# Two trunk layers on one core: GpSimd's elementwise work moves to VectorE, attention scores are computed over 128 rows, and the modulation products are shared out anew

## The chip, the cores and the metric

One core of one Trainium2 chip runs the whole program in one launch. The metric is device time in microseconds, from start to end of an execution; lower is better. TensorE (PE) multiplies, VectorE (DVE), ScalarE (ACT) and GpSimd (POOL) work elementwise, and SyncE (SP) only issues the transfers from and to memory (DMA).

## The reference, cut to what matters

384 tokens (256 latent, 128 context) of width 1024 pass through two layers. Everything is float32.

```python
def swiglu(h, w1, w3, w2):
    return (jax.nn.silu(h @ w1) * (h @ w3)) @ w2
...
m = jax.nn.silu(cond) @ w_mod[l] + b_mod[l]          # 9 vectors of 1024 for each layer and kind of token
...
h = swiglu(mod(x, 0), ffn1_w1[l], ffn1_w3[l], ffn1_w2[l])
x = layer_norm(ALPHA * x + 0.5 * m[:, :, 2] * h, ln_g[l, 0], ln_b[l, 0])
h, aux = mixer(mod(x, 1), l)
x = layer_norm(ALPHA * x + m[:, :, 5] * h, ln_g[l, 1], ln_b[l, 1])
h = swiglu(mod(x, 2), ffn2_w1[l], ffn2_w3[l], ffn2_w2[l])
x = layer_norm(ALPHA * x + 0.5 * m[:, :, 8] * h, ln_g[l, 2], ln_b[l, 2])
```

`mod(x, i)` is x(1+scale)+shift with two of the nine vectors. The mixer projects its input to pooling, to differential attention (4 heads with two softmax maps each), to neighbourhood attention (4 heads) and to three gate vectors, projects each branch to 1024 columns, adds them up under their gates and multiplies by `w_out`. Latent queries and keys of the differential attention are rotated (rope).

## The kernel before, in words

**High and low parts.** PE multiplies a rounded format (`fp32r`). Every operand of a large product is therefore split: ACT writes the rounded high part, another engine subtracts it and writes the low part, and `mm3` makes three passes (high by high, high by low, low by high). Weights come as 384 units of 128 x 1024 in one fixed order (`PLAN`), each loaded to `raw` by SP, rounded to `whi` by ACT and subtracted to `wlo` by DVE (`split_one`, L262). Ten split units are kept ahead of PE (`RING`).

**FFNs.** There are four, called FFN(layer, 0 or 1). A round j multiplies one unit each of `w1` and `w3` by the transposed input `xT` (24 passes of 384 columns each, into two banks `f`), then `glu` makes h on ACT and DVE, its high part `hhi` on ACT and its low part `hlo` on GpSimd. Up to round 16 a round also multiplies an earlier h by a unit of `w2` (18 passes of 512 columns into `acc`); the last six units of `w2` are kept for `tail`, which finishes one block of 128 tokens after the other, so that the layer norm of a block on DVE and ACT lies beside the products of the next. The first FFN begins inside `start`, which has an order of its own and computes the first 16 modulation columns.

**Modulation.** A product of the condition with 128 columns of `w_mod` (a "unit" of modulation) is done on DVE by two passes over 128 x 1024, one for each kind of token (`gemv_acc`, L306, tiles `wm` and `junk`). There are 128 units after the start. `gemv_quota` and `gemv_tick` spread them in the FFNs over "ticks" (one after each weight unit that PE uses up): 24 in each of three FFNs and 8 in the last, and each mixer takes 24.

**Residual.** `xa` keeps the normalised x without its gain and offset. `residual` (L415, L416) multiplies by the one and adds the other on GpSimd, three blocks after each layer norm but the last: in FFNs in rounds 7 to 9, in a mixer after the v projections (`rows_pass`, tile `v`).

**Mixers.** After the v projections a planner, `Jobs.emit`, takes jobs with an engine, a duration and dependencies, and fixes the order of the instructions on every engine. Priorities are `SIDE` (attention) before `UNIT` (projections, gates, output products, in their fixed order) before `SLOW` (modulation). Attention runs in 12 items with 384 keys and 6 with 128 keys for each mixer: scores (`ss`), maximum (DVE), exponential (ACT), transposes (`pt`), values (`o`). One item's scores are four passes: for each half e of a head pair one over 128 rows (`qa` holds the high part of q twice; `ka` holds the high and the low part of k) and one over 64 rows (`ql`, the low part of q, with the high part of k). q's low part and most of the rope (`u`, `kraw`) are GpSimd's, k's low part is DVE's. The chosen order is static: each engine runs its list and waits where an input is late.

Of the kernel before, what the change touches and what calls it, by code (L numbers as in the profile page):

```python
# [18 lines left out]
P = 128  # L19
# [5 lines left out]
HD = 64  # L25
# [27 lines left out]
MIX_LATENCY = 0.1, 2.0  # L53
SPLITS = 1
# [3 lines left out]
QK_LO = "GV"  # L58
# [50 lines left out]
class Jobs:  # L109
# [9 lines left out]

    def after(self, i, d):  # L120

        self.jobs[i][2].append(d)

    def emit(self, stock=None):
        n = len(self.jobs)
        rank = [0.0] * n
        for i in reversed(range(n)):
            rank[i] += self.jobs[i][1]
            for d in self.jobs[i][2]:
                rank[d] = max(rank[d], rank[i] + self.latency)  # L130
# [6 lines left out]
        while todo:  # L137
            best = None
            for i in todo:
# [3 lines left out]
                t = max([at.get(eng, 0.0)] + [end[d] + (self.dma_latency if self.jobs[d][0] == "D" else self.latency) for d in deps])  # L143
# [31 lines left out]
def trunk_kernel(ctx: ExitStack, tc: tile.TileContext, wst, wmod, wmod0, x_lat, x_ctx, cvec, cT,  # L175
# [4 lines left out]
    N_Q, N_S = 34, 21  # L180
# [305 lines left out]
    def tail(acc, accl, hT, keys, nk, gates, l, s):  # L486
# [67 lines left out]
        to_xT_ev(1, bs1, ab)  # L554
        t[2], nm[2] = ln_sum(2, acc[2], gates[1])
# [4 lines left out]
        pump(4 if s == 0 else 2)  # L560
# [8 lines left out]
    def glu(b1, b3, n, hT_hi, hT_lo):  # L569
        s = get("S", [P, n], F32, "s")  # L570
        S.activation(s, b1, AF.Silu)  # L571
        h = get("S", [P, n], F32, "h")
        V.tensor_tensor(h, s, b3, ALU.mult)  # L573
        S.copy(hT_hi, h)  # L574
        G.tensor_tensor(hT_lo, h, hT_hi.bitcast(F32), ALU.subtract)  # L575
        rel(s, h)

    def ffn(l, f, ctx_part, gate_at):
# [7 lines left out]
        j0 = N_ST if first else 2  # L586

# [7 lines left out]
        if first:  # L595
# [3 lines left out]
            gemv_quota(24, TICKS0)  # L599
        else:  # L600
            gemv_quota(min(24, len(gq)), TICKS * min(24, len(gq)))
            pair = [[take(w, l, f, h) for h in range(2)] for w in ("w1p", "w3p")]
            for c in range(2):
# [11 lines left out]
                glu(bb[0], bb[1], 256, hT[c][0][:, 0:256], hT[c][1][:, 0:256])  # L615
# [72 lines left out]
    def mix(l, ctx_part, H):  # L688
# [32 lines left out]
        gb = ln_rows(l, 0)  # L721
# [37 lines left out]
        n_gv = min(MIX_GEMV, len(gq))  # L759
# [37 lines left out]

        misc = [lambda: load("pool", 1.9, (band, cband),
# [31 lines left out]
        for i in range(first, last_u):  # L830
# [6 lines left out]
            d = add("A", .95, [raw_ld[i], d], split_hi, W_PRIO, need="W")  # L837
            d = u_lo[i] = add("V", 1.14, [d], lo, W_PRIO, free="R")
# [10 lines left out]
        def product(i, key, deps=()):  # L849
# [12 lines left out]
            for k0 in range(0, KC, PRODUCT_CUT):  # L862
                k1 = min(KC, k0 + PRODUCT_CUT)
                chain[0] = add("P", .49 * (k1 - k0), [u_lo[i], chain[0]] + list(deps), part(k0, k1), UNIT,
# [4 lines left out]
        d = None  # L869
        for k in gv:  # L870
# [10 lines left out]
            d = add("V", 1.16, [ld["wm", k], d], f0, SLOW)  # L881
            d = add("V", 1.16, [d], f1, SLOW, free="M")
# [13 lines left out]
        jobs.after(gate_d[0], add("A", .2, [d], f, free="B"))  # L896
# [31 lines left out]
        y_done = {}  # L928
        pT = [get("S", [P, T], F32, "pT") for _ in range(2)]
# [21 lines left out]
        for fc in range(2):  # L951
# [28 lines left out]
        def k_out(src, n, dep):  # L980
# [12 lines left out]
            return add("A", .2, [d], f, free="B")  # L993

        def to_y(kind, m, deps):
# [8 lines left out]
            def f():  # L1004
                box["y", kind, m] = get("S", [P, T], F32, "y")
                V.tensor_scalar(box["y", kind, m], box["yT", kind, m], gcol if kind == "b" else 1.0, None, ALU.mult)
                rel(box["yT", kind, m], ytok.pop((kind, m)))
            d = add("V", .53, [d], f, need="S", free="B S")

            def f():  # L1010
                out[m] = get("S", [P, T], F32R, "yhi"), get("S", [P, T], F32R, "ylo")
                S.copy(out[m][0], box["y", kind, m])
            d = add("A", .43, [d], f, need="S S")

            def f():
                G.tensor_tensor(out[m][1], box["y", kind, m], out[m][0].bitcast(F32), ALU.subtract)
                rel(box["y", kind, m])
            y_done[1 if kind == "b" else 2, m] = add("G", .98, [d], f, free="S")
# [626 lines left out]
```

## Time and profile before

| | us |
|---|---|
| median of 3 runs (1794.89 to 1797.36) | 1795.97 |
| the profiled execution's own time | 1795.24 |
| its span, first to last instruction | 1793.3 |

| engine | busy us | share of the span | instructions |
|---|---|---|---|
| PE matmuls | 1743.0 | 97% | 9444 |
| PE weight loads | 1619.8 | 90% | 9444 |
| DVE | 1254.2 | 70% | 1871 |
| ACT | 718.7 | 40% | 1234 |
| POOL | 365.3 | 20% | 263 |

PE is listed as busy nearly all the time, but its instructions overlap and their ends are modelled, so this share doesn't say that PE works at its full pace; the distance from one start to the next does. The other engines' shares are means over stages of different kinds: the start takes 68 us, FFN(0,0) ends at about 315, the first mixer at 638, FFN(0,1) at 906, FFN(1,0) at 1183, the second mixer at 1508.

### The profile page before, as it was taken

To read this page: it belongs to the slowest core of one execution; us is meant where nothing else is said; L and a number is where in the kernel's file an instruction comes from. 1 tells how busy PE (TensorE), PEld (TensorE's weight loads), DVE (VectorE), ACT (ScalarE), POOL (GpSimd) and SP (SyncE) were. 2 spreads that over 40 slices of the span, in tenths; PEclk is the share of its full clock that TensorE was granted. 3 is DMA by queue.
4 is the path that set the end of the run, shared out by engine and by line. 5 is a ranking of instruction groups with operands and counts; after the bars stand their busy time and mean duration, and the time that the engine had idled before them with its cause. 6 is when DMAs were issued, how large, how long until landed. Compare 5 with 4: busy or idle time off the path is not lost.

```text
span 1793.3 us, 24509 instructions
## 1 busy us (share of the span) xinstructions
PE 1743.0 (97%) x9444; PEld 1619.8 (90%) x9444; DVE 1254.2 (70%) x1871; ACT 718.7 (40%) x1234; POOL 365.3 (20%) x263
## 2 busy tenths in 40 slices
PE   7899999999999999999999999999999999999998
PEld 6799999788899999999999999978889999999997
DVE  6775656779988886776475776565998988665234
ACT  5532333355653362323353332334465445423231
POOL 4400000347210100410100320123540110023010
PEclk8999999999999999999999999999999999999999
DMA  8465553352446355465346465425244652653420
GB/s 320 143 238 186 186 188 118 105 216 95 147 177 238 138 209 197 167 223 191 118 149 223 157 223 201 153 72 183 103 143 144 250 206 99 233 176 132 143 102 35
DMA packets 88072, 301.65 MB, mean 168 GB/s; under 512 B 11058, under 2 KB 13970, under 8 KB 87956
## 3 DMA queue, kind: packets, MB, share of 16 engines
q1 hardware_dynamic: 87956, 300.09, 47.1%
q8 instruction: 74, 1.21, 0.3%
q14 instruction: 42, 0.34, 0.1%
HBM read 296.86 MB, written 3.19 MB: 167 GB/s over the span
## 4 chain that ended last, share of the span: by engine, by line
PE 84%; DVE 10%; issue 3%; ACT 1%; POOL 1%; DMA 1%; SPq 0%; DVEq 0%; ACTq 0%; POOLq 0%
PE f L214 38%; PE acc L214 24%; PE gt L214 11%; PE pj L214 4%; DVE junk L306 3%; DVE wlo L262 2%; PE v L214 2%; PE ss L214 1%; PE st L214 1%; PE f1c L214 1%; PE xTp L424 1%; DVE ka L1165 1%; PE o L214 1%; DVE u L1208 1%; DVE mx L1053 1%
## 5 line engine op out<-in xcount | busy, mean ns | idle before, releaser
L262 DVE TENSOR_TENSOR wlo<-raw,whi 128x1024 fp32r<-128x1024 f32 x379 | 488.9, 1317 | 153.8 <-ACT whi L257 153.4
L214 PE MATMUL f<-xT_hi,whi 128*128 128x384 f32 (+1 forms) x1344 | 445.2, 331 | 0.0
L214 PE MATMUL f<-xT_hi,wlo 128*128 128x384 f32 (+1 forms) x1344 | 444.9, 331 | 0.0
L214 PE MATMUL f<-xT_lo,whi 128*128 128x384 f32 (+1 forms) x1344 | 444.5, 331 | 0.0
L257 ACT CAST whi<-raw 128x1024 fp32r<-128x1024 f32 x384 | 384.2, 1047 | 11.1 <-DVE modcol L306 7.4
L306 DVE CUSTOM_DVE_ANT_0 junk<-wm,silu_bc 128x1024 bf16<-128x1024 f32 x256 | 350.7, 1370 | 3.5
L575 POOL TENSOR_TENSOR hlo<-h,hhi 128x384 fp32r<-128x384 f32 (+1 forms) x84 | 84.0, 1000 | 901.8 <-ACT hhi L574 901.8
L214 PEld LDWEIGHTS f<-xT_hi,whi 128*128 128x128 f32 x1344 | 252.7, 188 | 2.4
L214 PEld LDWEIGHTS f<-xT_lo,whi 128*128 128x128 f32 x1344 | 252.7, 188 | 2.4
L214 PEld LDWEIGHTS f<-xT_hi,wlo 128*128 128x128 f32 x1344 | 252.6, 188 | 0.0
L214 PE MATMUL acc<-whi,hlo 128*128 128x512 f32 x624 | 244.2, 391 | 0.0
L214 PE MATMUL acc<-wlo,hhi 128*128 128x512 f32 x624 | 244.0, 391 | 0.0
L214 PE MATMUL acc<-whi,hhi 128*128 128x512 f32 x624 | 244.0, 391 | 0.0
L573 DVE TENSOR_TENSOR h<-s,f 128x384 f32<-128x384 f32 (+1 forms) x84 | 45.7, 544 | 248.3 <-PE f L214 179.6
L574 ACT CAST hhi<-h 128x384 fp32r<-128x384 f32 (+1 forms) x84 | 42.5, 505 | 346.5 <-DVE h L573 346.5
L571 ACT ACTIVATE s<-f 128x384 f32<-128x384 f32 (+1 forms) x84 | 40.7, 484 | 262.0 <-PE f L214 261.9
L214 PEld LDWEIGHTS acc<-whi,hlo 128*128 128x128 f32 x624 | 117.1, 188 | 24.6
L214 PEld LDWEIGHTS acc<-whi,hhi 128*128 128x128 f32 x624 | 117.2, 188 | 22.8
L214 PEld LDWEIGHTS acc<-wlo,hhi 128*128 128x128 f32 x624 | 117.1, 188 | 22.8
L214 PE MATMUL gt<-xT_hi,whi 128*128 128x384 f32 x384 | 129.7, 338 | 0.0
L214 PE MATMUL gt<-xT_lo,whi 128*128 128x384 f32 x384 | 128.5, 335 | 0.0
L214 PE MATMUL gt<-xT_hi,wlo 128*128 128x384 f32 x384 | 128.5, 335 | 0.0
(236 smaller groups left out, 2370.9 us busy)
## 6 DMA issues: line engine op xcount, KB each, us to landing
raw<-in_wst SPq DMA_DIRECT2D x384, 512.0 KB, 3.7
wm<-in_wmod SPq DMA_DIRECT2D x128, 512.0 KB, 4.7
ld<-in_wmod SPq DMA_DIRECT2D x16, 512.0 KB, 9.5
gate<-gd SPq DMA_DIRECT2D x12, 512.0 KB, 3.9
lng<-in_lnrow SPq DMA_DIRECT2D x6, 512.0 KB, 3.9
lnb<-in_lnrow SPq DMA_DIRECT2D x6, 512.0 KB, 4.9
nab<-in_nabias SPq DMA_DIRECT2D x4, 512.0 KB, 7.3
out<-y SPq DMA_DIRECT2D x6, 256.0 KB, 2.0
```

The lines of the kernel that those rows point to most:

```text
L214: PE.matmul(out, a, b, start=start, stop=stop)
L257: S.copy(ws[i][0], raws[i])
L262: eng.tensor_tensor(ws[i][1], raw, ws[i][0].bitcast(F32), ALU.subtract)
L306: V.tensor_tensor_reduce(out=junk, in0=t, in1=silu_bc["t"][:, cd, :], scale=1.0, scalar=0.0, op0=ALU.mult, op1=ALU.add, accum_out=modcol[l ...
L424: PE.transpose(b[:, q, :], t[:, kc * P:(kc + 1) * P], ident)
L571: S.activation(s, b1, AF.Silu)
L573: V.tensor_tensor(h, s, b3, ALU.mult)
L574: S.copy(hT_hi, h)
L575: G.tensor_tensor(hT_lo, h, hT_hi.bitcast(F32), ALU.subtract)
L1053: V.reduce_max(mx, ss[:, :, :N], axis=AX.X)
L1165: KL.tensor_tensor(box["ka", kind, m][e][rs[1 - e], :], kt[rs[e], 0:384], box["ka", kind, m][e][rs[e], :].bitcast(F32), ALU.subtract)
L1208: V.tensor_tensor(u[0][o:o + 32, :], qT["b", m][i:i + 32, 0:256], rope[i:i + 32, 1, :], ALU.mult)
```

## The change

Five things are changed together.

1. Elementwise work leaves GpSimd in the FFNs and mixers: `hlo`, the residual, q's low part, the rope and the bias of the neighbourhood attention go to DVE. In `glu` the low part becomes a function `low`, which the FFN calls after the tick. The partner rows of the rope are copied out of PSUM by ACT (`rot`, four copies of 32 rows).
2. Scores: one tile `qs` holds the high part of q and its low part, each twice, so that both passes contract over 128 rows.
3. Modulation units: 42, 36, 36 and 8 in the four FFNs, 6 in the first mixer and 0 in the second.
4. In `tail` ahead of a mixer two weight units are split before the last block's layer norm, where all four were split after it.
5. The durations of the planner's jobs are other numbers, and it counts no delay between two jobs of one engine and a longer one behind PE (`PE_LAG`). The mixers' residual becomes six jobs of the lowest priority. The start is planned by the same rule, so some rows there change places.

```diff
-TICKS0, TICKS = 52, 2.1
+GEMV_TICKS = 52
+FFN_GEMV = {(0, 0): 42, (0, 1): 36, (1, 0): 36, (1, 1): 8}
-MIX_GEMV, MIX_AHEAD = 24, 10
+MIX_GEMV, MIX_AHEAD = (6, 0), 10
...
     def residual(ti, gb):
-        G.tensor_tensor(xa[ti], xa[ti], gb[0], ALU.mult)
-        G.tensor_tensor(xa[ti], xa[ti], gb[1], ALU.add)
+        for e, op in ((0, ALU.mult), (1, ALU.add)):
+            V.tensor_tensor(xa[ti], xa[ti], gb[e], op)
...
         to_xT_ev(1, bs1, ab)
+        if s == 0:
+            pump(2)
         t[2], nm[2] = ln_sum(2, acc[2], gates[1])
...
-        pump(4 if s == 0 else 2)
+        pump(2)
...
         V.tensor_tensor(h, s, b3, ALU.mult)
         S.copy(hT_hi, h)
-        G.tensor_tensor(hT_lo, h, hT_hi.bitcast(F32), ALU.subtract)
+        def low():
+            V.tensor_tensor(hT_lo, h, hT_hi.bitcast(F32), ALU.subtract)
+        return low
...
-                    glu(bb[0], bb[1], T, *hT[j])
+                    lows.append(glu(bb[0], bb[1], T, *hT[j]))
                     rel(*bb)
                 tick()
+                while lows:
+                    lows.pop(0)()
...
-                        mm(o, qq[:, t * P:(t + 1) * P], kk, True, False)
-                        mm(o, ql[r, t * P:(t + 1) * P], kk[r, :], False, True)
+                        for h in range(2):
+                            mm(o, qq[:, h, :], kk, h == 0, h == 1)
...
-            d = add("A", .95, [raw_ld[i], d], split_hi, W_PRIO, need="W")
-            d = u_lo[i] = add("V", 1.14, [d], lo, W_PRIO, free="R")
+            d = add("A", 1.05, [raw_ld[i], d], split_hi, W_PRIO, need="W")
+            d = u_lo[i] = add("V", 1.35, [d], lo, W_PRIO, free="R")
```

On DVE at the end of FFN(0,0), the rows from the last round's h to the first row of the tail stand so before (`junk` is one modulation pass; the last round's `hlo` stands on POOL):

```order
L573 TENSOR_TENSOR h_2422<-s_2420,f_418_2393 128x384
L262 TENSOR_TENSOR wlo_2427<-raw_2356,whi_2426 128x1024
L306 ISA junk,modcol_72<-wm_2360,silu_bc 128x1024
L306 ISA modcol_72 128x1
L306 ISA junk,modcol_72<-wm_2360,silu_bc 128x1024
L306 ISA modcol_72 128x1
L314 TENSOR_TENSOR modcol_72<-modcol_72,bmod 128x16
```

and so in the changed kernel:

```order
L581 TENSOR_TENSOR h_2497<-s_2495,f_436_2468 128x384
L268 TENSOR_TENSOR wlo_2501<-raw_2425,whi_2500 128x1024
L312 ISA junk,modcol_72<-wm_2466,silu_bc 128x1024
L312 ISA modcol_72 128x1
L312 ISA junk,modcol_72<-wm_2466,silu_bc 128x1024
L312 ISA modcol_72 128x1
L586 TENSOR_TENSOR hlo_2494<-h_2497,hhi_2493 128x384
```

The last round's `hlo` now stands on DVE behind one weight split and one modulation unit. In FFN(0,1) and FFN(1,0) only the weight split stands between, and in FFN(1,1) nothing.

On DVE in the tail of FFN(0,0), just ahead of the first mixer, the last block's layer norm (from `r` to `xa`) and the four weight splits behind it stand so before:

```order
L453 TENSOR_TENSOR xT_lo<-y_2621,xT_hi 128x4x128 x2
L396 TENSOR_TENSOR r_2634<-acc_750,gate_1840 128x512
...
L558 TENSOR_SCALAR xa_94<-r_2634,nm_2640,rs_2643 128x1024
L262 TENSOR_TENSOR wlo_2655<-raw_2391,whi_2654 128x1024
L262 TENSOR_TENSOR wlo_2661<-raw_2430,whi_2660 128x1024
L262 TENSOR_TENSOR wlo_2667<-raw_2658,whi_2666 128x1024
L262 TENSOR_TENSOR wlo_2673<-raw_2664,whi_2672 128x1024
```

and so in the changed kernel:

```order
L459 TENSOR_TENSOR xT_lo<-y_2695,xT_hi 128x4x128 x2
L268 TENSOR_TENSOR wlo_2709<-raw_2462,whi_2708 128x1024
L268 TENSOR_TENSOR wlo_2715<-raw_2504,whi_2714 128x1024
L402 TENSOR_TENSOR r_2720<-acc_756,gate_1889 128x512
...
L566 TENSOR_SCALAR xa_94<-r_2720,nm_2726,rs_2729 128x1024
L268 TENSOR_TENSOR wlo_2741<-raw_2712,whi_2740 128x1024
L268 TENSOR_TENSOR wlo_2747<-raw_2718,whi_2746 128x1024
```

Two splits moved ahead of the layer norm.

On PE in the first mixer, an item's scores stand so before, with the row before and after them:

```order
L214 MATMUL o_3199<-va_2681,pT_3181 128x64
L214 MATMUL ss_3202<-ka_3061,qa_3048 128x384
L214 MATMUL ss_3202<-ka_3061,ql_3187 128x384
L214 MATMUL ss_3202<-ka_3062,qa_3049 128x384
L214 MATMUL ss_3202<-ka_3062,ql_3187 128x384
L983 MATMUL kt_3219<-ident,kc_2885 128x128
```

and so in the changed kernel:

```order
L220 MATMUL o_3439<-va_2755,pT_3390 128x64
L220 MATMUL ss_3454<-ka_3239,qs_3323 128x384 x2
L220 MATMUL ss_3454<-ka_3240,qs_3323 128x384 x2
L1098 MATMUL pt_3463<-ident,p_3393 128x128
L1098 MATMUL pt_3464<-ident,p_3394 128x128
```

The count of passes stays; the two of 64 rows are gone.

## Rows read from the trace of the kernel before

**Rows 1.** Stages: us, busy us (instructions) of PE, PEld, DVE, ACT, POOL; PEclk; DMA

```profile
364.50:503.00 138.50, 132.06 (x747) 118.14 (x745) 125.60 (x230) 79.48 (x202) 61.09 (x52) 0.99 0.42 151
638.00:906.00 268.00, 268.00 (x1481) 253.13 (x1480) 174.62 (x231) 93.43 (x130) 41.74 (x28) 1.00 0.51 178
...
1234.00:1372.00 138.00, 131.21 (x743) 117.75 (x741) 125.71 (x229) 79.13 (x202) 61.21 (x52) 0.99 0.42 150
```

**Rows 2.** Chain of waits, 378 to 455 us (shares), 453 to 457.5 us (start, us)

```profile
by line: DVE wlo L262 17.9%; DVE junk L306 15.4%; issue 12.3%; DVE ka L1165 9.2%; DVE u L1208 7.7%; DVE mx L1053 6.2%; PE kb L214 5.5%; DVE ss L1052 3.3%; DVE ytok L1112 3.2%; DVE mx L1048 2.6%; DVE p L1072 2.6%; DVE cf L1071 1.9%; DVE mx L
...
455.29 0.67 PE o L214 x6
```

**Rows 3.** Chain of waits of the whole span, in FFN(0,1): start, us, what

```profile
773.29 8.34 PE f L214 x48
781.63 4.12 PE acc L214 x18
...
848.20 41.62 PE f L214 x240
```

**Rows 4.** Lines L262 and L306: count, ns min/median/max, first and last start

```profile
L262 DVE TENSOR_TENSOR wlo<-raw,whi x379: 1207/1220/3428, 15.2 to 1745.7; 128x1024 fp32r<-128x1024 f32 x190
...
L306 DVE CUSTOM_DVE_ANT_0 junk<-wm,silu_bc x256: 1208/1222/3424, 99.9 to 1595.3; 128x1024 bf16<-128x1024 f32 x128
```

**Rows 5.** Timeline where the mixers begin: start, us, engine, line, what [idle before]

```profile
333.91 2.84 DVE L558 TENSOR_SCALAR xa<-r,nm,rs 128x1024 f32<-128x1024 f32 x1
336.67 4.49 DVE L262 TENSOR_TENSOR wlo<-raw,whi 128x1024 fp32r<-128x1024 f32 x2
...
328.98 2.40 POOL L415 TENSOR_TENSOR xa<-xa,lng 128x1024 f32<-128x1024 f32 x1 [28.18 <-DMA lng<-in_lnrow]
...
336.28 2.67 POOL L416 TENSOR_TENSOR xa<-xa,lnb 128x1024 f32<-128x1024 f32 x1
...
340.08 0.50 PE L214 MATMUL v<-wlo,xT_hi 128*128 128x512 f32 x1 [4.24 <-DVE wlo L262]
...
1209.14 0.79 PE L214 MATMUL v<-wlo,xT_hi 128*128 128x512 f32 x1 [4.40 <-DVE wlo L262]
```

**Rows 6.** Stretches behind those two waits, columns as in rows 1

```profile
340.60:344.00 3.40, 3.40 (x9) 2.64 (x9) 2.83 (x3) 0.00 (x0) 0.00 (x0) 0.50 0.44 154
...
1209.10:1214.40 5.30, 5.26 (x12) 4.13 (x13) 3.39 (x3) 0.00 (x0) 0.00 (x0) 0.50 0.42 140
```

**Rows 7.** Timeline of PE, one item's scores, up to the next instruction

```profile
478.09 0.34 PE L214 MATMUL ss<-ka,qa 128*128 128x384 f32 x1
478.36 0.44 PE L214 MATMUL ss<-ka,ql 64*128 64x384 f32 x1
...
479.46 0.55 PE L1082 MATMUL pt<-ident,p 128*128 128x128 f32 x3
```

**Rows 8.** Groups on DVE, 364.5 to 503 us: busy us, mean ns | idle before

```profile
L306 DVE CUSTOM_DVE_ANT_0 junk<-wm,silu_bc 128x1024 bf16<-128x1024 f32 x21 | 31.3, 1491 | 0.1
```

**Rows 9.** Groups on POOL, whole span, columns as in rows 8

```profile
L415 POOL TENSOR_TENSOR xa<-xa,lng 128x1024 f32<-128x1024 f32 x15 | 45.0, 3001 | 75.8 <-DMA lng<-in_lnrow 56.5 <-PE xTp L424 19.3
```

**Rows 10.** Timeline at the end of FFN(0,0), DVE, ACT, POOL and PE

```profile
298.54 0.55 DVE L573 TENSOR_TENSOR h<-s,f 128x384 f32<-128x384 f32 x1 [1.40 <-PE f L214]
300.69 1.23 DVE L262 TENSOR_TENSOR wlo<-raw,whi 128x1024 fp32r<-128x1024 f32 x1 [1.59 <-ACT whi L257]
301.83 1.22 DVE L306 CUSTOM_DVE_ANT_0 junk<-wm,silu_bc 128x1024 bf16<-128x1024 f32 x1
...
304.36 0.17 DVE L314 TENSOR_TENSOR modcol<-modcol,bmod 128x16 f32<-128x16 f32 x1
...
299.61 1.05 ACT L257 CAST whi<-raw 128x1024 fp32r<-128x1024 f32 x1
...
299.78 1.01 POOL L575 TENSOR_TENSOR hlo<-h,hhi 128x384 fp32r<-128x384 f32 x1 [7.31 <-ACT hhi L574]
...
302.14 0.39 PE L214 MATMUL acc<-whi,hlo 128*128 128x512 f32 x1
```

More of the change, by code (lines that the diff above doesn't have):

```diff
@@ L863, in product @@
                 k1 = min(KC, k0 + PRODUCT_CUT)
[L864 removed]
+                chain[0] = add("P", .52 * (k1 - k0), [u_lo[i], chain[0]] + list(deps), part(k0, k1), UNIT,
                                need="" if k0 else "B", free="W" if k1 == KC else "")
             return chain[0]
[L869 removed]
+        d = v5 = None
         for k in gv:
@@ L895, in f @@
             rel(box["gT"])
-        jobs.after(gate_d[0], add("A", .2, [d], f, free="B"))
+        jobs.after(gate_d[0], add("A", .25, [d], f, free="B"))
+        d = ld["gb"]
+        for ti in range(3):
+            for e, op in ((0, ALU.mult), (1, ALU.add)):
+                def f(ti=ti, e=e, op=op):
+                    V.tensor_tensor(xa[ti], xa[ti], box["gb"][e], op)
+                    if (ti, e) == (2, 1):
+                        rel(*box["gb"])
+                d = add("V", 1.25, [d], f, SLOW, free="W" if (ti, e) == (2, 1) else "")
         neglam = cst.tile([P, 1], F32, tag=f"neglam{l}", name=f"neglam{l}")
@@ L1002, in to_y @@
             d = add("P", .4, deps, f, need="B")
[L1004 to L1018, printed above, removed]
+            split_y((1 if kind == "b" else 2, m), out, m, lambda: box["yT", kind, m], lambda: gcol if kind == "b" else 1.0, d,
+                    lambda: rel(box["yT", kind, m], ytok.pop((kind, m))), "B S")
         def item(kind, m, t, ready):
@@ L1147, in fq @@
             def fq():
-                qa = box["qa", kind, m] = [get("S", [P, 256], F32R, "qa") for _ in range(2)]
+                qs = box["qs", kind, m] = get("Q", [P, 2, 2, 256], F32R, "qs")
                 for e in range(2):
                     for r in rs:
-                        S.copy(qa[e][r, :], qT[kind, m][rs[e], 0:256])
+                        S.copy(qs[r, e, 0, :], qT[kind, m][rs[e], 0:256])
             def fk():
@@ L1230, in mix, with rotate, f @@
-            r = add("G", 1.4, [d], f, free="S S S" + " S" * (m == 3))
+                    S.copy(p[o:o + 32, :], b[i:i + 32, 0:256])
+                rel(b)
+            return add("A", 2.1 if key == "q" else 2.4, [dep], f, need="S S", free="B")
+        for m in range(4):
+            q = evac_pair("q", m, product(unit("qb", l, m), ("qb", m)))
+            k = evac_pair("k", m, product(unit("kb", l, m), ("kb", m)))
+            ko = k_out(kb_t(m)[:, 384:512], m, k)
+            def rotate(key, m=m):
+                def f():
+                    x = qT["b", m][:, 0:256] if key == "q" else box["kraw", m]
+                    out = x if key == "q" else kb_t(m)[:, 0:256]
+                    p = box["p" + key, m]
+                    V.tensor_tensor(p, p, rope[:, 1, :], ALU.mult)
+                    V.tensor_tensor(x, x, rope[:, 0, :], ALU.mult)
+                    V.tensor_tensor(out, x, p, ALU.add)
+                    rel(p)
+                    if key == "k":
+                        rel(x)
+                        if m == 3:
+                            rel(rope)
+                return f
+            r = add("V", 1.3, [q, ld["rope"]], rotate("q"), free="S")
+            r = add("V", 1.3, [k, r], rotate("k"), free="S S" + " S" * (m == 3))
```

177 lines of the change are left out of this document (82 added, 95 removed).

## The prediction

> **What bounds the kernel now.** I read the stages first, then the chain of waits in the stage where PE falls behind, then timelines at the places that the change touches. In an FFN the chain is PE alone: 24 passes of 384 columns take 4.17 us (0.174 us each), 18 of 512 columns take 4.12 us (0.229 each), and one stretch follows the other without a gap [rows 3]. Nothing on DVE, ACT or POOL shortens that. In the attention stage of a mixer it is different. There DVE is busy for 125.6 of 138.5 us [rows 1], and the chain from 378 to 455 us runs almost wholly over DVE: weight splits 18%, modulation passes 15%, score and rope pieces behind them [rows 2]. PE is listed at 132.1 us there, but count its work at full pace: 12 projections and 7 gates of 24 passes and 6 products of 6 are 492 passes of 384 columns at 0.174, so 85.6 us; 48 score passes would be 8.4 us at that pace; the other 207 of its 747 instructions start about 0.11 us apart when nothing holds them (0.67 us for 6) [rows 2], so 23 us. That is 117 us of work in 138.5 us, and the same in the second mixer's 138.0 us [rows 1]. So DVE bounds this stage, and up to 21.5 us per mixer can be had there.
>
> DVE is slow for two reasons. It does much, and it is held up: a weight split takes 1.22 us in the median and up to 3.43, a modulation pass 1.22 and up to 3.42 [rows 4]; the long ones lie beside GpSimd instructions [rows 5].
>
> **The change, part by part.**
>
> *Start of the mixers.* PE waited 4.24 and 4.40 us for a weight split [rows 5]. The split was late because the layer norm before it was: the residual ran on GpSimd from 328.98 to 338.95 us, and beside it the normalising step took 2.84 us (two-input passes of that width take 1.22 where nothing holds them) and two splits took 4.49 instead of 2.44 [rows 4, 5]. Now GpSimd is empty and two of the four splits stand ahead of the layer norm. They delay it by 2.4 us and the missing blocks give back 1.6 in the normalising step alone; the next two splits are needed only two units later, 12 passes of 0.23 us. So both waits should go. Behind them PE's granted clock stood at 0.50, the 1.2 GHz level, for 3.4 and 5.3 us [rows 6], which costs half of that, 1.7 and 2.6 us. Gain 4.24 + 4.40 + 1.7 + 2.6 = 12.9 us; between 6 (a wait of half the length stays) and 13.
>
> *Score passes.* An item's four passes take 478.09 to 479.46, so 1.37 us, where four at 0.174 would take 0.70; a full pass before a 64-row one is held too (0.27) [rows 7]. 24 items in two mixers: 0.67 x 24 = 16 us of PE time. Between 0 and 16, and part of the room counted above, not on top of it. The Trainium skill (TensorE: Matmul & The Clock Gate, section "Why this matters for your kernels") says that a matmul over fewer contraction rows takes the same time as one over 128; by that this edit gains nothing, and the rows here, at about twice the time of a full pass, don't agree.
>
> *VectorE's load in the attention stage.* Removed: 21 modulation passes of 1.49 us and their reads, about 33 us [rows 8]; the blocks on what stays. Added, with 0.42 us for 256 columns (a straight line through 0.55 for 384 and 1.22 for 1024 [rows 4, 10]): q's low part 12 x 0.42 = 5, rope 24 pieces instead of 16, so 3.4, bias 2 x 1.22 = 2.4, together 11 us. That leaves about 104 of 138.5 us. In the first mixer 2 modulation units (5 us) and the residual (6 x 1.22 = 7.3 us, which cost GpSimd 3.0 each [rows 9]) are put in between at lowest priority. So DVE falls to some 104 to 116 us, PE's 117 us become the floor, and ACT (79.5 us [rows 1]) gains rope and score copies and stays below both. The gain lies between 5 us per mixer (score passes where PE doesn't wait today, 7 or 8 of 12 items) and 21.5 (PE never waits). Three engines at 75 to 95% under static lists won't reach the floor; I take three quarters, 16 us per mixer, 32 in all.
>
> *FFNs.* GpSimd's blocks cost nothing here today (PE didn't wait), so nothing is gained. What is added: `hlo` (0.55 us for 1.01) and more modulation. One round of FFN(0,0) on DVE: h 0.55, then a wait of 1.60 until ACT has done `hhi` and the next weight's high part, splits at 1.14, `hlo` 0.58, modulation units at 2.53 [rows 10]. With 42 units in 52 ticks: 0.55 + 1.60 + 3 x 1.14 + 0.58 + 2.42 x 2.53 = 12.3 us against PE's 8.34 + 4.12 = 12.46: just fits. In the last five rounds, without `w2`, PE takes 8.32 (41.62 / 5) [rows 3]; DVE needs 10.1 us with two units and 7.5 with one. The skipped ticks fall so that three of the last four steps have two: h comes late by 1.7, 1.0, 2.7 and at last 4.4 us. PE doesn't feel that before the tail. There it wants the last `hlo` at 302.14, and GpSimd had it at 300.79 [rows 10]. Now: h starts 298.54 + 4.4 = 302.9, then 0.55 + 1.60 + 1.14 + 2.53 + 0.55 = 6.4, so 309.3, a wait of 7.2 us, and a spell at half clock of the kind above (1.7). Without the lateness the wait would be 2.8. I take 8 us lost, between 3 and 11. In FFN(0,1) and FFN(1,0) units stop five ticks before the end, the lateness is worked off, and `hlo` stands behind one split: 298.54 + 0.55 + 1.60 + 1.14 + 0.55 = 302.4, so 0.3 us lost each. The residual's 2.4 us in rounds 7 to 9 are covered by the ten units ahead of PE; without that cover they would cost up to 7 us in each.
>
> *Start, and the units' transfers.* The start's list changes by a few rows: nothing in sum, within plus or minus 2 us (one or two passes of 1.22 [rows 4] earlier or later). The extra `wm` loads raise the traffic in the FFNs, where DMA engines were busy half of the time [rows 1]: nothing.
>
> *Sum.* 12.9 + 32 - 8 - 0.6 = 36 us. Against the profiled execution's 1795.24 (span 1793.3 and 1.9 around it, 0.7 under the median of 1795.97): 1759.
>
> **Rivals.**
>
> *The attention stage stays slow.* ACT gets four copies of 32 rows for each of q and k and a second copy of q's low part, and scores wait for that longer way; only one item's scores fit at a time. For it: in 138.5 us ACT had only 79.5 busy, but it stands in every link. Against it: the chain was DVE's. Then 5 us per mixer: 12.9 + 10 - 8.6 = 14 gained, 1781.
>
> *Modulation finds its place in FFN(0,0) after all* (the lateness doesn't build up, or the last rounds have more slack): 5 to 7 us better, 1753.
>
> *Score passes stay as slow as now*, as by the skill's rule. For it: PE's first pass of an item is long too, which 64 rows alone wouldn't explain. Against it: every 128-row pass elsewhere starts 0.174 after the last. PE's floor rises by 8 us per mixer to 125; three quarters of 13.5 are 10 each, so 1771.
>
> *Slower: VectorE becomes the bound of three FFNs.* If the long passes on DVE aren't GpSimd's doing, a modulation pass stays at its mean of today (1.37, with read 1.45) and a split at 1.32 in the FFNs. Then a round of FFN(0,0) takes 0.55 + 1.60 + 4.0 + 0.58 + 2.42 x 2.9 = 13.7, 1.3 over PE's, and its last five 10.0 against 8.32: 13 x 1.3 + 5 x 1.7 = 25 us, with some 8 at the end; FFN(0,1) and FFN(1,0) lose 5 to 8 each, and in the mixers 32 shrinks to some 16. 12.9 + 16 - 33 - 13 = 17 slower, 1812. It decides from the point where a round on DVE takes longer than PE's 12.46. Against it: the medians of 1.22 lie at the minimum [rows 4], so most instances are unhindered.
>
> **How the numbers follow.** Forecast (mixers gain most, FFN(0,0) pays) 0.55, 1748 to 1770, likeliest 1759; modulation finds its place 0.14, 1753 and down to 1743; attention stays slow 0.16, about 1781 and up to 1788; scores stay slow 0.06, 1771; slower 0.06, 1800 to 1812; no change within 0.2% 0.03. A change of 0.2% (3.6 us) is about the least that can be told here. So faster 0.91, same 0.03, slower 0.06. The range of 1742 to 1786 leaves out the slower case, the unchanged one and the ends of two others.
>
> **What would show it.** Right: no wait of PE for `wlo` at `v`; an item's score passes in about 0.7 us; weight splits and modulation passes outside the start all near 1.22 us; 364 to 503 us shrinks by 10 to 20 with DVE's share lower; a PE wait of 3 to 8 us for `hlo` at the end of FFN(0,0), with the clock at 0.5 behind it, and hardly any in the next two. Wrong: gaps between `f` and `acc` inside FFNs; PE waiting for ACT's copies in attention; score passes at 0.35 us as today.

## The result

The changed kernel takes 1766.43 us (median of 4 runs, 1763.96 to 1768.49) against 1796.01 for the kernel before (4 runs, 1794.89 to 1797.36): ratio 0.9834, 95% interval 0.9817 to 0.9851. That is 29.6 us less; 36 less, 1759, were forecast. The profiled execution, the slowest of the four, took 1768.49 us with a span of 1766.8.

To see where the time went, the trace was read through PE's starts. For two matmuls that follow each other, the distance between their starts, less the distance at full pace for that width (0.1735 us for 384 columns, 0.227 for 512, 0.120 for 256, 0.109 for 128, 0.084 for 64), is time that PE lost, be it a wait, a half clock or a slow pass. Gaps under 25 ns are left out. Added up by stage (us; attention is the 138 us from the first `qc` on):

| kernel | start | end of FFN(0,0) | mixers begin | attention 1 | attention 2 | mixers end | FFN(0,1), FFN(1,0) begin | rest | lost | span |
|---|---|---|---|---|---|---|---|---|---|---|
| before | 31.3 | 0.2 | 13.4 | 26.8 | 27.0 | 1.5 | 0.3 | 0.9 | 101.4 | 1793.3 |
| changed | 33.4 | 8.6 | 0.2 | 9.1 | 13.5 | 1.7 | 6.7 | 1.5 | 74.7 | 1766.8 |
| difference | 2.1 | 8.5 | -13.2 | -17.7 | -13.5 | 0.2 | 6.3 | 0.6 | -26.7 | -26.5 |

The span less the lost time is 1692 us in both, and within 0.6 us of that in every kernel below. So nothing else moved: PE does the same work, and only its gaps changed. The forecast had the signs and sizes of four columns; it missed the begin of two FFNs, and the experiments show that the cause it gave for the attention columns was only partly right.

**Where the mixers begin** the waits of [rows 5] are gone; the chain of waits of the changed kernel shows 72 passes of 0.227 us without a gap in all four places:

```profile
335.30 16.32 PE v L220 x72
352.49 16.35 PE v L220 x72
...
1188.00 16.32 PE v L220 x72
1205.20 16.33 PE v L220 x72
```

Weight splits and modulation passes, over the whole span (count, ns min/median/max; [rows 4] before), have lost their long cases:

```profile
L268 DVE TENSOR_TENSOR wlo<-raw,whi x379: 1203/1219/1887, 15.2 to 1719.0; 128x1024 fp32r<-128x1024 f32 x190
...
L312 DVE CUSTOM_DVE_ANT_0 junk<-wm,silu_bc x256: 1201/1222/1228, 100.8 to 1569.1; 128x1024 bf16<-128x1024 f32 x128
```

**Attention**, columns as in [rows 1]. These are windows of 134 us beside the 138 us of [rows 1]. DVE is down from 125.6 to 110 and 102 us, and ACT is up from 79 to 99:

```profile
369.00:503.00 134.00, 133.20 (x820) 130.00 (x819) 109.77 (x229) 99.24 (x249) 0.00 (x0) 1.00 0.42 147
1221.60:1356.00 134.40, 132.00 (x800) 127.32 (x799) 101.79 (x221) 99.07 (x253) 0.00 (x0) 0.99 0.37 130
```

The windows don't hold the same list of work: more of PE's instructions lie in these 134 us than in the 138 before, 820 and 800 against 747 and 743. The last score pass starts 135.9 and 129.9 us behind the first `qc`, where it was 138.0 and 138.3. (That the listed busy time of PE hardly differs shows again that it doesn't measure pace.) An item's four score passes in PE's timeline start 0.79 us ahead of the next instruction, where [rows 7] had 1.37:

```profile
473.78 0.94 PE L220 MATMUL ss<-ka,qs 128*128 128x384 f32 x4
474.57 0.38 PE L220 MATMUL o<-vb,pT 128*128 128x128 f32 x2
```

**The end of FFN(0,0)**, in DVE's and PE's timelines and in the stretch behind (columns of [rows 1]); [rows 10] has the same place before:

```profile
303.71 0.55 DVE L581 TENSOR_TENSOR h<-s,f 128x384 f32<-128x384 f32 x1
305.78 1.23 DVE L268 TENSOR_TENSOR wlo<-raw,whi 128x1024 fp32r<-128x1024 f32 x1 [1.52 <-ACT whi L263]
306.92 1.22 DVE L312 CUSTOM_DVE_ANT_0 junk<-wm,silu_bc 128x1024 bf16<-128x1024 f32 x1
...
309.33 0.55 DVE L586 TENSOR_TENSOR hlo<-h,hhi 128x384 fp32r<-128x384 f32 x1
...
304.85 0.50 PE L220 MATMUL acc<-whi,hhi 128*128 128x512 f32 x1 [0.93 <-ACT hhi L582]
...
309.94 0.80 PE L220 MATMUL acc<-whi,hlo 128*128 128x512 f32 x1 [4.35 <-DVE hlo L586]
...
310.50:315.60 5.10, 5.10 (x13) 3.97 (x12) 0.00 (x0) 0.00 (x0) 0.00 (x0) 0.50 0.27 99
```

h was forecast for 302.9 and comes at 303.71; `hlo` was forecast done at 309.3 and is done at 309.88. The two waits and the stretch at half clock make 8.5 us. These times agree better than the terms behind them: PE itself runs 2.1 us later here than before (its last `f` pass starts at 300.15, before at 298.07). Against PE, h is late by 3.1 us and not by 4.4.

**Where FFN(0,1) and FFN(1,0) begin** there is a wait that the forecast didn't have. The chain of waits, DVE's and PE's timelines, and the stretch behind the second of them:

```profile
644.66 7.23 DMA wm<-in_wmod
...
645.33 5.76 DVE L268 TENSOR_TENSOR wlo<-raw,whi 128x1024 fp32r<-128x1024 f32 x5 [0.52 <-ACT whi L263]
651.91 1.22 DVE L312 CUSTOM_DVE_ANT_0 junk<-wm,silu_bc 128x1024 bf16<-128x1024 f32 x1 [0.82 <-DMA wm<-in_wmod]
...
654.33 0.75 DVE L586 TENSOR_TENSOR hlo<-h,hhi 128x256 fp32r<-128x256 f32 x2
...
654.80 0.50 PE L220 MATMUL acc<-whi,hlo 128*128 128x512 f32 x1 [1.64 <-DVE hlo L586]
...
935.45 0.50 PE L220 MATMUL acc<-whi,hlo 128*128 128x512 f32 x1 [2.52 <-DVE hlo L586]
...
935.50:940.00 4.50, 4.50 (x13) 3.58 (x14) 2.54 (x6) 3.41 (x6) 0.00 (x0) 0.64 0.34 138
```

DVE waits for the first modulation chunk, and the low parts of the first two h stand behind it (of PE's first wait of 1.64 us the transfer explains at most DVE's 0.82; the rest is the unit's own two passes). 36 units in 52 ticks are 0.69 a tick, so the first unit falls on the second tick; 24 units in 50 ticks were 0.48, and it fell on the third.

### The profile page after: what moved, and what is told of

It is laid out like the page before. It is cut to its first block, busy times and chain, and to the rows that moved or that the text cites. A ratio compares the mean times of both kernels' runs of the same rounds, so it can differ in the third digit from the quotient of the medians.

```text
span 1766.8 us, 24383 instructions
## 1 busy us (share of the span) xinstructions
PE 1726.4 (98%) x9444; PEld 1621.3 (92%) x9444; DVE 1245.9 (71%) x2045; ACT 751.3 (43%) x1322; POOL 37.4 (2%) x21
## 4 chain that ended last, share of the span: by engine, by line
PE 91%; DVE 4%; DMA 2%; ACT 1%; issue 1%; SPq 0%; DVEq 0%; ACTq 0%
PE f L220 36%; PE acc L220 24%; PE gt L220 11%; PE v L220 4%; PE pj L220 4%; DVE junk L312 2%; PE qb L220 2%; PE kb L220 2%; PE o L220 1%; PE ss L220 1%; PE st L220 1%; PE f1c L220 1%; PE qc L220 1%; PE kc L220 1%; DMA wm<-in_wmod 1%
## 5 line engine op out<-in xcount | busy, mean ns | idle before, releaser
L268 DVE TENSOR_TENSOR wlo<-raw,whi 128x1024 fp32r<-128x1024 f32 x379 | 456.8, 1222 | 166.7 <-ACT whi L263 166.0
L312 DVE CUSTOM_DVE_ANT_0 junk<-wm,silu_bc 128x1024 bf16<-128x1024 f32 x256 | 312.5, 1221 | 6.8 <-DMA wm<-in_wmod 2.5
L220 PEld LDWEIGHTS gt<-xT_hi,wlo 128*128 128x128 f32 x384 | 72.7, 189 | 2.0 <-DVE wlo L268 2.0
```

The costliest lines, as they stand in the source:

```text
L220: PE.matmul(out, a, b, start=start, stop=stop)
L268: eng.tensor_tensor(ws[i][1], raw, ws[i][0].bitcast(F32), ALU.subtract)
L312: V.tensor_tensor_reduce(out=junk, in0=t, in1=silu_bc["t"][:, cd, :], scale=1.0, scalar=0.0, op0=ALU.mult, op1=ALU.add, accum_out=modcol[l ...
```

## The experiments

Each is one edit to the changed kernel unless it says otherwise. The table gives medians, ratios to the kernel before with their intervals, and PE's lost time by stage as above.

| run | us | ratio | end of FFN(0,0) | mixers begin | attention 1, 2 | mixers end | FFNs begin |
|---|---|---|---|---|---|---|---|
| changed | 1766.43 | 0.9834 (0.9817 to 0.9851) | 8.6 | 0.2 | 9.1, 13.5 | 1.7 | 6.7 |
| e1 | 1752.39 | 0.9753 (0.9738 to 0.9768) | 0.3 | 0.2 | 9.1, 13.5 | 1.7 | 0.3 |
| e2 | 1794.66 | 0.9988 (0.9979 to 0.9997) | 4.7 | 0.2 | 16.1, 15.7 | 30.4 | 0.3 |
| e3 | 1782.55 | 0.9924 (0.9909 to 0.9939) | 8.4 | 0.2 | 16.2, 21.2 | 2.9 | 4.2 |
| e4 | 1773.32 | 0.9868 (0.9853 to 0.9882) | 8.3 | 8.4 | 9.2, 12.0 | 1.5 | 4.3 |
| e5 | 1766.85 | 0.9831 (0.9814 to 0.9847) | 8.3 | 0.2 | 9.1, 13.5 | 1.7 | 6.4 |
| e6 | 1762.57 | 0.9807 (0.9792 to 0.9822) | 8.6 | 0.2 | 9.1, 13.4 | 1.7 | 0.3 |
| e7 | 1753.54 | 0.9758 (0.9742 to 0.9775) | 0.9 | 0.2 | 9.1, 13.5 | 1.7 | 0.6 |
| e8 | 1764.91 | 0.9821 (0.9807 to 0.9836) | 8.5 | 0.2 | 11.4, 12.2 | 1.5 | 4.3 |
| e11 (before, new shares) | 1794.94 | 0.9993 (0.9984 to 1.0003) | 1.0 | 12.3 | 24.6, 22.2 | 5.7 | 0.3 |
| e13 | 1765.41 | 0.9827 (0.9810 to 0.9843) | 8.5 | 0.2 | 9.7, 13.0 | 1.6 | 4.1 |
| e10 | 1750.65 | 0.9749 (0.9734 to 0.9764) | 0.3 | 0.2 | 9.1, 12.0 | 1.6 | 0.5 |
| e12 | 1771.56 | 0.9866 (0.9851 to 0.9881) | 0.3 | 0.2 | 21.7, 20.1 | 1.9 | 0.3 |

**e1: the low part ahead of the tick.**

```diff
-                tick()
                 while lows:
                     lows.pop(0)()
+                tick()
```

> The changed kernel with one thing turned round: in every FFN round the low part of h stands on DVE ahead of the weight split and the modulation units of that tick, not behind them. Theory: the 8.4 us that PE loses at the end of FFN(0,0) and the 6.2 us at the starts of FFN(0,1) and FFN(1,0) are lost because the low part stands behind a split and a modulation unit (at the starts behind a unit whose transfer is late), so about 1.2 us stay at the end (h itself is late), under 1 us at the starts, and the time falls by 12 to 13.5 us, to some 1753. Rival: DVE simply has too much to do there, and the order only moves the lateness: within 2 us of 1766.

14.0 us faster, a little more than expected: not 1.2 us but 0.3 us stay at the end of FFN(0,0). DVE's timeline there shows why:

```profile
301.53 0.55 DVE L581 TENSOR_TENSOR h<-s,f 128x384 f32<-128x384 f32 x1
302.65 0.56 DVE L586 TENSOR_TENSOR hlo<-h,hhi 128x384 fp32r<-128x384 f32 x1 [0.58 <-ACT hhi L582]
303.61 1.22 DVE L268 TENSOR_TENSOR wlo<-raw,whi 128x1024 fp32r<-128x1024 f32 x1 [0.40 <-ACT whi L263]
```

Behind h DVE has to wait for ACT anyway (1.52 us in the changed kernel), and `hlo` now fills a part of that. The round is shorter by that much (h to h 9.39 us, from 292.14, where it was 9.86, from 293.85), so the lateness is smaller too. The order was the cause, not the amount of work.

**e6: the first unit put off.**

```diff
             gemv_quota(FFN_GEMV[l, f], min(GEMV_TICKS, 2.1 * FFN_GEMV[l, f]))
+            pace["n"] = -1.0
```

> The changed kernel with the first modulation unit of FFN(0,1), FFN(1,0) and FFN(1,1) put off to a later tick, so that the low parts of the first h stand ahead of it on DVE. Theory: the waits of PE for the low part at the starts of FFN(0,1) and FFN(1,0) come from the transfer of the first modulation chunk, 7 to 8 us, for which DVE waits with the low parts behind it; they go, 1.9 + 4.4 us with the half clock behind the second, and the time falls by 6 us to 1760. Rival: the splits ahead of it (5 x 1.15 us) make DVE late there, with or without the unit: the waits stay at 1 us or more, 1764 to 1766.

The column falls from 6.7 to 0.3 and the median by 3.9 us. In DVE's timeline the low parts follow the five splits at once, 3.7 us earlier than in the changed kernel (3.3 when counted from the first of the splits):

```profile
644.95 5.77 DVE L268 TENSOR_TENSOR wlo<-raw,whi 128x1024 fp32r<-128x1024 f32 x5 [0.52 <-ACT whi L263]
650.63 0.75 DVE L586 TENSOR_TENSOR hlo<-h,hhi 128x256 fp32r<-128x256 f32 x2
```

So the splits alone don't make them late. That the median falls by less than the profile's 6.3 has a reason in the table: in e3, e4, e8 and e13, which leave this place as it is, the column is 4.1 to 4.3, and in e5, which leaves it too, 6.4. In the changed kernel's profiled execution the second wait is 0.9 us longer than in those four, and passes at half clock behind it lose another 1.5; e5 has the same behind its first wait. So some 2.4 of the 6.7 us don't come in every execution.

**e7: the low part of h on GpSimd again.**

```diff
-            V.tensor_tensor(hT_lo, h, hT_hi.bitcast(F32), ALU.subtract)
+            G.tensor_tensor(hT_lo, h, hT_hi.bitcast(F32), ALU.subtract)
```

> The changed kernel with the low part of h in the FFNs on GpSimd again, as before; all else as in the changed kernel. Theory: in FFNs the move to DVE cost and gave nothing: the waits at the end of FFN(0,0) and at two FFN starts go almost wholly, 12 to 14 us faster, 1753. The price: about 80 GpSimd instructions of 1 us stand beside DVE's passes again, so single splits and modulation passes take up to 2.2 us. Rival: with 42 units in FFN(0,0) DVE has no room for these blocks, PE waits inside the rounds or longer at the end, and the time stays at 1764 or rises to 1772.

1753.54, 12.9 us faster and 1.2 above e1 (four runs each, which don't overlap; the profiles put 0.9 of it at the ends and begins of the FFNs). So for the FFNs the engine hardly matters; what stands ahead of the low part does. The price that was expected didn't come: the longest split is 1.89 us in both kernels.

**e4 and e5: the two halves of the mixers' begin.** e4 has the mixers' residual on GpSimd at its old place (and its six jobs on DVE taken out); e5 has all four splits behind the layer norm.

```diff
         rows_pass("va", va_t, 2)
+        for ti in range(3):
+            for e, op in ((0, ALU.mult), (1, ALU.add)):
+                G.tensor_tensor(xa[ti], xa[ti], gb[e], op)
```

> The changed kernel with the residual of the mixers on GpSimd again, at its old place behind the first v products; all else stays. Theory: the waits where the mixers begin had two causes, GpSimd beside the layer norm and four splits behind it; with two splits ahead of the layer norm the blocks are mostly hidden: a wait of 0 to 3 us in each mixer comes back, and the attention stage gains up to 2 us in each from 7 us less on DVE: 1764 to 1770. Rival: GpSimd alone was the cause, so both waits of over 4 us come back with their half clock: 1774 to 1779.

```diff
-        if s == 0:
-            pump(2)
         t[2], nm[2] = ln_sum(2, acc[2], gates[1])
...
-        pump(2)
+        pump(4 if s == 0 else 2)
```

> The changed kernel with all four weight splits behind the last layer norm of the tail again, GpSimd still empty. Theory: without GpSimd beside them the layer norm and the splits are 1.6 and 2 us shorter than before, so of the waits of 4.24 and 4.40 us some 0.6 us stay in each, too short for a drop of the clock: 1767 to 1769. Rival: the place of the splits was the cause: waits of 2.5 to 4.4 us with half clock, 1773 to 1779.

e4 loses 4.2 us in each mixer, e5 nothing at all. In e4's timelines of DVE, GpSimd and PE:

```profile
329.17 0.16 DVE L417 TENSOR_TENSOR rs<-rs,nt 128x1 f32<-128x1 f32 x1
...
337.67 0.69 DVE L403 CUSTOM_DVE_ANT_0 r<-r,xa 128x512 f32<-128x512 f32 x1
...
339.01 2.43 DVE L403 CUSTOM_DVE_ANT_0 r<-r,xa 128x512 f32<-128x512 f32 x1
343.97 2.10 DVE L417 TENSOR_TENSOR rs<-rs,nt 128x1 f32<-128x1 f32 x1
...
338.49 2.40 POOL L743 TENSOR_TENSOR xa<-xa,lng 128x1024 f32<-128x1024 f32 x1 [251.73 <-DVE su L403]
...
350.26 0.50 PE L220 MATMUL v<-wlo,xT_hi 128*128 128x512 f32 x1 [2.19 <-DVE wlo L268]
...
1204.08 0.50 PE L220 MATMUL v<-wlo,xT_hi 128*128 128x512 f32 x1 [2.33 <-DVE wlo L268]
```

The step `r<-r,xa` on 512 columns takes 0.69 us alone and 2.43 beside GpSimd, and a step on one column 2.10 instead of 0.16. The Trainium skill (SBUF — State Buffer, section "Who interferes with whom") says that a VectorE instruction with two inputs from SBUF contends with a GpSimd instruction that reads SBUF, and that the port pair they share is locked exclusively; both of these rows have two inputs, and they agree. GpSimd was the cause, and with GpSimd empty the place of the splits is worth nothing. With GpSimd at work two splits ahead of the norm go with about half the wait (2.2 and 2.3 us for 4.24 and 4.40 in [rows 5]); the two kernels differ in more than that, so that the place of the splits does this is not shown.

**e3: the second score pass over 64 rows again.** The product of the two low parts is left out; ACT's copies stay.

```diff
-                        for h in range(2):
-                            mm(o, qq[:, h, :], kk, h == 0, h == 1)
+                        mm(o, qq[:, 0, :], kk, True, False)
+                        mm(o, qq[r, 1, :], kk[r, :], False, True)
```

> The changed kernel with the second score pass over the 64 rows of q's low part and k's high part again (the product of the two low parts is left out); the copies that ACT makes for the 128-row form stay. Theory: an item's four passes take 1.37 us again where they took about 0.7, and because PE is close to its floor in the attention stages, most of the 0.67 x 24 = 16 us shows: 10 to 16 us slower, 1776 to 1782. Rival (a pass over 64 rows takes the same time as one over 128, and PE's slow passes came from elsewhere): within 2 us of 1766.

16.1 us slower. The attention columns and the mixers' ends grow by 7.1, 7.7 and 1.2, together 16.0. In PE's timeline an item stands 1.46 us ahead of the next instruction, where it was 0.79:

```profile
478.18 1.53 PE L220 MATMUL ss<-ka,qs 128*128 128x384 f32 x4
479.64 0.49 PE L220 MATMUL o<-vb,pT 128*128 128x128 f32 x2
```

0.67 x 24 = 16.1. The rule of the Trainium skill (TensorE: Matmul & The Clock Gate, section "Why this matters for your kernels"), by which a pass over fewer rows takes the same time, doesn't hold for these passes of 64 rows among passes of 128; the whole price shows. Whether the 64 rows are slow or the change between the two forms is, no run here separates.

**e8: the planner's old numbers** (old durations where a job was there before, and one delay between any two jobs).

```diff
-        return self.dma_latency if eng == "D" else 0.0 if eng == by else self.latency + PE_LAG * (eng == "P")
+        return self.dma_latency if eng == "D" else self.latency
...
-            d = add("V", .9 if cx else 1.25 if df else 2.1, ...
+            d = add("V", .5 if cx else 1. if df else 1.6, ...
```

> The changed kernel with the planner's old numbers where a job was there before (durations, and one delay between any two jobs); the jobs themselves stay. Theory: the measured durations matter little where PE is near its floor: the attention stages lose 0 to 6 us each, the start, which is planned by the same rule, gets its 2 to 3 us back: 1764 to 1775. Rival: the order by measured durations made the attention stage fast: 10 us or more lost in each, 1784 and up.

1764.91: the measured durations gain nothing that can be told. One attention stage is 2.3 us worse, the other 1.3 better, the start 2.2 better (31.2 against 33.4; the kernels with the changed start have 32.4 to 33.4).

**e2 and e11: the shares of modulation, each way.** e2 is the changed kernel with the old shares, e11 the kernel before with the new ones.

```diff
-FFN_GEMV = {(0, 0): 42, (0, 1): 36, (1, 0): 36, (1, 1): 8}
+FFN_GEMV = {(0, 0): 24, (0, 1): 24, (1, 0): 24, (1, 1): 8}
 PRODUCT_CUT = 8
-MIX_GEMV, MIX_AHEAD = (6, 0), 10
+MIX_GEMV, MIX_AHEAD = (24, 24), 10
```

> The changed kernel with the old shares of modulation units: 24, 24, 24 and 8 in the FFNs, 24 in each mixer. Theory: VectorE's load in the attention stages falls mostly by the units that left: back there they are about 21 passes of 1.33 us with their reads, 28 us, and PE's lost time in the attention stages (about 9 and 13 us now) grows by 8 to 14 us in each; in the FFNs the waits at the end of FFN(0,0) and at two starts shrink, 8 to 13 us back. In sum 1766 to 1782, 1773 likeliest, with the growth visible in the two stages. Rival: the blocks of GpSimd and the short score passes alone made the attention stage fast: it stays as it is and only the FFN waits go, 1753 to 1757.

> The kernel before with one part of the change, the new shares of modulation units (42, 36, 36, 8; 6 and 0 in the mixers). Theory: in the attention stages DVE loses some 28 us of passes, so PE's lost time there falls from 26.8 us to 15 to 20 in each; the waits of 4 us for a weight split where the mixers begin stay, since GpSimd still has its work; the FFNs lose at most 2 us, since the low part of h stands on GpSimd: 1772 to 1782. Rival: GpSimd's long chain (q's low part, rope, bias) bounds the attention stages, not DVE's load: they stay as they are, and the time is 1794 to 1797.

Both miss the range of their theory; e11 lies in that of its rival (1794 to 1797). Everything but the shares is worth 1.8 us, the shares alone 1.1 (the interval reaches from 2.9 faster to 0.5 slower), both together 29.6. In e2 the attention stages are still 22 us better than before, but 30.4 us are lost at the ends of the mixers, a place that the forecast didn't consider. DVE's and PE's timelines of e2 there:

```profile
617.16 1.22 DVE L922 TENSOR_TENSOR xa<-xa,lnb 128x1024 f32<-128x1024 f32 x1
618.29 1.22 DVE L312 CUSTOM_DVE_ANT_0 junk<-wm,silu_bc 128x1024 bf16<-128x1024 f32 x1
...
620.57 1.22 DVE L312 CUSTOM_DVE_ANT_0 junk<-wm,silu_bc 128x1024 bf16<-128x1024 f32 x1
...
622.43 0.68 DVE L402 TENSOR_TENSOR r<-acc,gate 128x512 f32<-128x512 f32 x1
...
628.77 1.97 PE L430 MATMUL xTp<-ident,xa 128*128 128x128 f32 x8 [7.16 <-DVE xa L537]
```

Modulation and residual have the lowest priority, so what doesn't fit into the mixer piles up at its end, and the tail's layer norm stands behind it. (The kernel before, with the same shares, loses 1.5 us there; which of the other edits fills DVE there was not run apart.) In e11 DVE is relieved, in the first attention stage from 125.6 to 103.3 us, and hardly anything follows:

```profile
364.00:503.00 139.00, 134.74 (x760) 121.20 (x759) 103.31 (x195) 79.24 (x203) 60.09 (x52) 0.98 0.35 119
```

PE's lost time falls by 2.2 and 4.8 us in the two stages, and the mixers' ends take back 4.2. The trace shows what the loss in these stages is made of. Sorted by kind (us, first and second mixer), with a wait counted where PE stood idle for more than 0.1 us:

| kernel | score passes over 384 keys | waits | other 384-column passes that lose 0.10 to 0.25 us (mostly half clock) | all else, small |
|---|---|---|---|---|
| before | 8.9, 8.7 | 7.4, 7.8 | 2.0, 2.3 | 8.5, 8.2 |
| changed | 0.9, 1.1 | 1.0, 3.0 | 1.3, 3.4 | 5.9, 6.0 |
| e3 | 8.3, 8.8 | 0, 2.5 | 1.4, 3.3 | 6.5, 6.6 |
| e11 | 9.0, 8.7 | 4.7, 3.2 | 1.8, 2.3 | 9.1, 8.0 |

New shares alone shorten the waits, but the waits were only 15 of 54 us. In e11's first stage one wait makes up most of what is left, and it ends with ACT and not with DVE (total us, times, longest):

```profile
PE o L215 <- ACT pT L1089: 2.9, 1, 2.9
```

**e13: q's low part and the rope's products on GpSimd again**, in the new form of the rope.

```diff
-                    V.tensor_tensor(p, p, rope[:, 1, :], ALU.mult)
-                    V.tensor_tensor(x, x, rope[:, 0, :], ALU.mult)
-                    V.tensor_tensor(out, x, p, ALU.add)
+                    G.tensor_tensor(p, p, rope[:, 1, :], ALU.mult)
+                    G.tensor_tensor(x, x, rope[:, 0, :], ALU.mult)
+                    G.tensor_tensor(out, x, p, ALU.add)
```

q's low part changes its engine in the same way.

> The changed kernel with q's low part and the three products and sums of the rope on GpSimd again (24 of them and 12 low parts of two pieces each in a mixer's attention stage); 128-row scores and the new shares of modulation stay. Theory, after the runs in which the old shares gave back everything and the new shares alone gave nothing: the attention stage had two bounds side by side, DVE's load and the chain over GpSimd. Then the chain comes back with DVE at 85 of 134 us or less, and PE's lost time in the attention stages rises from 9.1 and 13.5 us by 5 to 12 us in each: 1776 to 1790. Rival: it was DVE's load with the short score passes alone, GpSimd is harmless where DVE has room: the stages stay within 3 us in sum, 1763 to 1769.

The theory fell and its rival held: 1765.41, no change, with GpSimd busy for 29.4 us of the stage:

```profile
369.00:503.00 134.00, 132.78 (x826) 129.39 (x824) 101.51 (x197) 101.03 (x258) 29.39 (x36) 1.00 0.43 147
```

DVE's busy time falls with it, from 109.8 to 101.5 us, so this shows that the exchange costs nothing, not that GpSimd holds up no instruction of DVE.

**e10 and e12: versions that go on.** e10 is e1 with the start planned by the old rule of delays; e12 is e10 with `W_PRIO = 0`.

> The changed kernel with two edits: the low part of h ahead of the tick, and the start planned by the old rule of delays. Theory: the first edit gives 14 us (1752.4), the start gets back what PE lost there more than before (33.4 against 31.3 us), 2 us: 1750.3. Rival: the start's 2 us come from something else than the delays: 1752.

> The kernel of the run before it (low part ahead of the tick, old start) with the weight splits of the mixers at the priority of the attention work, not below it. Theory: part of what PE still loses in the attention stages (9.1 and 13.5 us) are waits for a split that stands behind attention work on ACT (2.0 us with the half clock behind it in the second mixer); these go, but attention's own links get later: 2 to 4 us faster or no change, 1746 to 1751. Rival: ACT, at 99 us of 134, is too full, and splits ahead of attention make the chain of an item longer: 3 us slower or more, 1753 to 1760.

e10 is the fastest kernel of the study, 45 us under the kernel before and 15.8 under the changed one; its step over e1 (1.7 us) is less than can be told here. Its profile doesn't put that step where the theory had it: the start loses 0.4 us less than in e1, and the second attention stage 1.5 less, in passes at half clock. In e12 12.6 and 8.1 us more are lost in the two stages than in e10, and 1771.56 lies beyond its rival's range of 1753 to 1760. In the first stage, where e10 waits for ACT once for 0.8 us, PE now waits for ACT's exponentials above all:

```profile
PE gt L223 <- ACT p L1080: 2.9, 2, 1.8
PE ss L223 <- ACT p L1080: 2.4, 1, 2.4
```

This fits the rival's mechanism, splits ahead of attention's links on ACT, at a higher price than it gave.

## Why the prediction was right, and where not

**Start of the mixers: 12.9 forecast, 13.2 measured.** The blocks by GpSimd were the cause (e4). That the two splits ahead of the norm help was wrong for the changed kernel (e5). The forecast counted the blocks on the normalising step and on two splits; steps on one column, which take 0.22 and 0.16 us alone, were held as well. Before, they stand on DVE beside GpSimd's residual:

```profile
329.68 1.72 DVE L409 SCALAR_TENSOR_TENSOR nt<-rs,v 128x1 f32<-128x1 f32 x1
...
331.62 2.25 DVE L411 TENSOR_TENSOR rs<-rs,nt 128x1 f32<-128x1 f32 x1
```

**Score passes: 16 of PE time forecast, 16.0 measured** (e3), all of it on the path.

**Attention: 32 forecast, 31.2 measured, for a reason that holds only in part.** The step "So DVE bounds this stage" failed: with 22 us taken off DVE the stage was 2.2 us faster (e11). PE stood idle for only 7.4 and 7.8 us in the two stages before, and in the first of them 2.6 us of the waits ended with ACT (total us, times, longest):

```profile
PE pt L1082 <- ACT p L1061: 2.6, 2, 1.8
PE pt L1082 <- DVE p L1072: 2.3, 2, 1.3
PE o L214 <- DVE pT L1088: 1.2, 1, 1.2
```

Of the 31.2 us, the score passes are 14.8 (e3), which had been counted as a part of DVE's room and came from PE itself. The shares alone are 7.0 (9.2 when undone in the changed kernel). The engine of q's low part and of the rope is nothing (e13), the planner's numbers about nothing (e8). That leaves some 7 to 9 us: by kind, about 4 us of waits and as much in small losses. No run here separates what took them off: the partner rows copied by ACT in place of 32-row products on GpSimd, the bias, or the low parts of the branch outputs. This stays open. That three quarters of the counted room came out right is luck: the room was well counted, but it wasn't DVE's.

**The shares pay at another place.** With the other edits made, they are worth 28.2 us (1794.66 to 1766.43), because without them 30.4 us are lost at the ends of the mixers. The forecast had 2 modulation units and the residual "put in between at lowest priority" and didn't ask what happens to such jobs if there is no room in between.

**End of FFN(0,0): 8 lost forecast, 8.5 measured**, by the forecast's own chain: late h, then split, unit and `hlo`. Two of its terms were off and made up for each other: the waits are 0.93 and 4.35 us where 7.2 was forecast, since h is less late, and the stretch at half clock costs some 2.7 where 1.7 was. At the ends of FFN(0,1) and FFN(1,0) PE loses 0.3 us each, as forecast.

**Begin of FFN(0,1) and FFN(1,0): nothing forecast, 6.3 lost.** The failed step is "The extra `wm` loads raise the traffic in the FFNs [...]: nothing". It looked at the mean load of the DMA engines; what counted was when the first chunk is asked for (behind four weight loads, landing 7.23 us after its issue) and that `hlo` stands behind the unit that waits for it. The start lost 2.1 us, a little beyond the bound of 2 that was given; about 1.0 of it is a longer stretch at half clock (from 71 to 73 us the granted clock was 0.50, before 1.00). These two make most of the miss of the profiled execution: 1768.49 less 1759 is 9.5, of which 6.3 and 2.1. The median misses by 7.4.

**The rivals.** ACT in attention (1781) didn't come: PE waited there for ACT for 0.8 us in the first stage and as long in the second. Score passes didn't stay slow (0.79 us), and modulation didn't find its place in FFN(0,0) without loss. VectorE as the bound of three FFNs didn't come either: PE lost 0.1 to 0.3 us inside the rounds of each.

## What to carry to other kernels

Write up PE's lost time by stage from its starts, for every version: here it splits a difference of a few us into places, where busy shares show nothing. When an in-order engine gets more work, look at what stands behind each instruction that can wait, for a transfer above all, and put what the bounding engine wants next ahead of it: one moved line gave 14 us. Two edits that give 1.1 and 1.8 us alone gave 29.6 together here, so undo one from the end and do one from the start before either is called useless.

## What the hardware showed unexpectedly

A VectorE step on one column took 2.10 us beside GpSimd where it takes 0.16 (e4), yet 29 us of GpSimd work on 256 columns inside attention, taken off DVE, cost nothing on balance (e13). Four score passes over 64 and 128 rows in turn took 1.46 us, four over 128 rows 0.79. Behind a wait of 1.64 us PE kept its full pace; behind one of 2.52 the granted clock was 0.64 over the next 4.5 us in the changed kernel's execution, and four kernels that leave the same place as it is lost about 2.4 us less at these two starts.
